# A small first transfer ahead of the large loads, with its results stored in mid-run

## The chip, the cores and the metric

The kernel runs on one core of a Trainium2 chip. The metric is the device time of one execution in microseconds (us). Each kernel was run several times, always beside runs of the kernel before on the same chip. A difference in time under 2% is called a difference only where its 95% interval leaves out 1. The span of a profile is shorter than the device time of the same run (before: 161.4 and 162.92 us).

## The reference

```python
# x: (32, 512, 1024) float32, 67.1 MB
def reference(x):
    relu_x = np.maximum(x, 0)
    return np.sum(relu_x, axis=-1).astype(np.float32)    # (32, 512)
```

There are 16384 rows of 4 KB. Each gives one output number, 4 bytes. Almost all the work is reading 67.1 MB.

## The kernel before

Partition `p` owns 128 consecutive rows, `128 p` to `128 p + 127`. They are loaded in seven large transfers of 16 rows a partition (8 MB each) into three buffers, then a tail of 8, 4, 2 and 1 rows and two half rows. All transfers are issued from one sequencer (SP) and so stand in one queue, served by 16 DMA engines.

```python
xv = x.rearrange("b s d -> (b s) d").rearrange("(p j) d -> p j d", p=P)     # P = 128
ov = out.rearrange("b s -> (b s)").rearrange("(p j) -> p j", p=P)
...                                                                         # cut: buffers, semaphores
for c in range(NBIG + 1):                    # NBIG = 7 large loads, NB = 3 buffers
    if c >= NB:
        sp.wait_ge(s_dve, 3 * (c - NB + 1))  # the buffer's last use is over
    if c < NBIG:
        sp.dma_start(out=buf[:, c % NB, :, :],
                     in_=xv[:, c * BIG : (c + 1) * BIG, :]).then_inc(s_in[c], 16)
...                                          # cut: tail loads of 8, 4, 2, 1 rows and two half rows
                                             # cut: ScalarE does relu, VectorE sums; late rows are
                                             #      done whole on one engine or the other
sp.wait_ge(s_tdve, 1)
sp.dma_start(out=ov[:, :], in_=res[:, :]).then_inc(s_out, 16)   # 128 pieces of 512 bytes
sp.wait_ge(s_out, 16)
```

Of the kernel before, what the change touches and what calls it, by code (L numbers as in the profile page):

```python
# [2 lines left out]

P = 128
D = 1024
BIG = 16
NBIG = 7
NTWO = 6
NB = 3
STEPS = [4, 5, 7]  # L10
MIXED = [3, 4, 5]
TAIL = [8, 4, 2, 1]
LAST = [512, 512]


def bass_relu_sum_kernel(
    nc: bass.Bass,
    x: bass.AP,
    out: bass.AP,
):  # L20





    fp32 = mybir.dt.float32
    ALU = mybir.AluOpType
    AF = mybir.ActivationFunctionType
    X = mybir.AxisListType.X

    B, S, _ = x.shape
    J = B * S // P
    assert BIG * NBIG + sum(TAIL) + 1 == J and sum(LAST) == D

    xv = x.rearrange("b s d -> (b s) d").rearrange("(p j) d -> p j d", p=P)
    ov = out.rearrange("b s -> (b s)").rearrange("(p j) -> p j", p=P)

    buf = nc.alloc_sbuf_tensor("buf", [P, NB, BIG, D], fp32)
    last = nc.alloc_sbuf_tensor("last", [P, LAST[1] + 1], fp32)
    res = nc.alloc_sbuf_tensor("res", [P, J], fp32)  # L40

    n_in = NBIG + len(TAIL) + 2
    s_in = [nc.alloc_semaphore(f"s_in{i}") for i in range(n_in)]
    s_act = nc.alloc_semaphore("s_act")
    s_dve = nc.alloc_semaphore("s_dve")
    s_tact = nc.alloc_semaphore("s_tact")
    s_tdve = nc.alloc_semaphore("s_tdve")
    s_out = nc.alloc_semaphore("s_out")

    sp, act, dve = nc.sync, nc.scalar, nc.vector  # L50


    tb = NBIG % NB
    for c in range(NBIG + 1):
        if c >= NB:
            sp.wait_ge(s_dve, 3 * (c - NB + 1))
        if c < NBIG:
            sp.dma_start(  # L58
                out=buf[:, c % NB, :, :], in_=xv[:, c * BIG : (c + 1) * BIG, :]
            ).then_inc(s_in[c], 16)  # L60
    r = 0
    tail = []
    for i, n in enumerate(TAIL):
        sp.dma_start(  # L64
            out=buf[:, tb, r : r + n, :],
            in_=xv[:, NBIG * BIG + r : NBIG * BIG + r + n, :],
        ).then_inc(s_in[NBIG + i], 16)
        tail.append((r, n, s_in[NBIG + i]))
        r += n
    sp.dma_start(  # L70
        out=buf[:, tb, r, 0 : LAST[0]], in_=xv[:, J - 1, 0 : LAST[0]]
    ).then_inc(s_in[-2], 16)
    sp.dma_start(out=last[:, 0 : LAST[1]], in_=xv[:, J - 1, LAST[0] : D]).then_inc(
        s_in[-1], 16
    )


    def on_act(t, acc):
        return act.activation(t, t, AF.Relu, accum_out=acc)  # L79

    def on_dve(t, acc):
        return dve.tensor_scalar(  # L82
            out=t, in0=t, scalar1=0.0, scalar2=None, op0=ALU.max, op1=ALU.add, accum_out=acc
        )

    def row(c, i):
        return buf[:, c % NB, i, :], res[:, c * BIG + i : c * BIG + i + 1]

    for c in range(NTWO):
        b, steps = c % NB, STEPS if c < NTWO - 1 else MIXED  # L90
        act.wait_ge(s_in[c], 16)
        if steps is MIXED:
            dve.wait_ge(s_in[c], 16)
            for i in (BIG - 4, BIG - 3):
                on_dve(*row(c, i))
        r = 0
        for i, n in enumerate(steps):
            t = buf[:, b, r : r + n, :]
            act.activation(t, t, AF.Relu).then_inc(s_act, 1)  # L99
            dve.wait_ge(s_act, 3 * c + i + 1)  # L100
            dve.tensor_reduce(  # L101
                out=res[:, c * BIG + r : c * BIG + r + n], in_=t, axis=X, op=ALU.add
            ).then_inc(s_dve, 1)
            r += n
        if steps is MIXED:
            for i in (BIG - 2, BIG - 1):
                on_act(*row(c, i))


    j0 = NBIG * BIG  # L110
    for c in range(NTWO, NBIG):
        act.wait_ge(s_in[c], 16)
        dve.wait_ge(s_in[c], 16)
        for i in range(BIG):
            (on_act if i % 2 else on_dve)(*row(c, i))
    for r, n, s in tail:
        if n > 1:
            act.wait_ge(s, 16)
        dve.wait_ge(s, 16)
        for i in range(r, r + n):  # L120
            f = on_act if (i - r) % 2 else on_dve
            f(buf[:, tb, i, :], res[:, j0 + i : j0 + i + 1])

    act.wait_ge(s_in[-2], 16)
    on_act(buf[:, tb, BIG - 1, 0 : LAST[0]], last[:, LAST[1] : LAST[1] + 1]).then_inc(s_tact, 1)
    dve.wait_ge(s_tact, 1)
    dve.wait_ge(s_in[-1], 16)
    on_dve(last[:, :], res[:, J - 1 : J]).then_inc(s_tdve, 1)


    sp.wait_ge(s_tdve, 1)
    sp.dma_start(out=ov[:, :], in_=res[:, :]).then_inc(s_out, 16)
    sp.wait_ge(s_out, 16)


# [1 line left out]
_INS = ['x']  # L137
_OUTS = [((32, 512), 'float32')]


# [21 lines left out]
```

## Time and profile before

| | before |
|---|---|
| time, median of 6 runs beside the changed kernel's | 162.87 us (162.65 to 163.22) |
| span of the profile | 161.4 us |
| share of the 16 DMA engines' time that is busy | 97.0% |
| VectorE, ScalarE busy | 76%, 63% |
| one 64 KB packet on one DMA engine, usual | 2.418 us |
| the 16 engines' first packets start | 1.73 to 2.97 us |
| last load lands (its 16 engines, first to last) | 158.05 to 158.92 us |
| last store, from issue to landing | 1.54 us |

These numbers come from the results, from the page, and from two kinds of records in the trace: packets (a packet is one piece that one DMA engine moves) and semaphore steps. A transfer's landing is 16 semaphore steps, one an engine, and it counts only when the last has come. Landings here and below are read from those steps; of a store they are called its confirmations. No view of the profile prints single packets and steps; a packet record doesn't name its engine, and an engine's first packets are told by which packet follows on which.

From the page of the kernel before: busy time of the compute engines, the DMA row (busy share in 40 equal slices, in tenths), what the DMA engines moved in each slice, and the queue with its packets, MB and share of 16 engines' time.

```profile
DVE 122.0 (76%) x56; ACT 101.0 (63%) x55; POOL 0.2 (0%) x4
...
DMA  7969979979979979979979979979979979899992
GB/s 260 504 292 504 471 341 487 487 325 487 487 325 487 471 309 520 471 309 520 487 309 504 487 325 487 487 325 487 487 325 487 487 325 487 374 422 414 406 406 74
...
q1 hardware_dynamic: 2016, 67.18, 97.0%
```

The DMA engines hardly pause from the first slice to the last. The GB/s row jumps up and down because a packet is counted in the slice in which it starts; three slices (12.1 us) together are steady. In the middle the kernel moves 16 x 65536 bytes / 2.418 us = 434 GB/s. The Trainium skill ("DMA: Bandwidth & Descriptors", Specifications) gives 435 GB/s as the ceiling of the fabric on the side of SBUF (the on-chip memory that the loads go to); the trace agrees.

From the chain of waits of the kernel before in order of time (start, duration, what):

```profile
1.16 41.26 DMA buf<-in_x_dram
...
64.16 36.40 DMA buf<-in_x_dram
...
124.16 34.13 DMA buf<-in_x_dram
158.29 0.02 issue
158.31 0.73 ACT buf L79 x2
159.04 0.02 issue
159.07 0.69 DVE last L82 x2
```

A DMA step in this chain runs from a transfer's issue to its landing and so contains the time in which it waited in the queue. The piece of 36.40 us is the fifth large load, which lands at 100.56 us.

From the DMA issues of the same kernel (KB, then us from issue to landing; for the seven large loads the median, which holds their wait in the queue too):

```profile
buf<-in_x_dram SPq DMA_DIRECT2D x7, 36.4
out_dram<-res SPq DMA_DIRECT2D x1, 64.0 KB, 1.5
```

### The profile page before, as it was taken

The numbers are of one execution on the slowest core, as the hardware profiler recorded it, in microseconds if no ns is written. First come the engines' busy times: TensorE is split into PE (matmuls) and PEld (weight loads), VectorE is DVE, ScalarE is ACT, GpSimd is POOL, SyncE is SP. The second block draws the span as 40 slices with busy tenths as digits, with TensorE's granted clock in tenths as the row PEclk, the third lists the DMA queues.
The fourth block names the chain that finished last, engine by engine and source line by source line (L and its number), as shares of the span: only waits on it lengthen the run. The fifth ranks groups of instructions, "written<-read, shape, count | busy, mean of one in ns | idle before, by whom it ended". The sixth has DMA issues, their size and how long they took to land.

```text
span 161.4 us, 143 instructions
## 1 busy us (share of the span) xinstructions
DVE 122.0 (76%) x56; ACT 101.0 (63%) x55; POOL 0.2 (0%) x4
## 2 busy tenths in 40 slices
DVE  0000003998969898798979989699899999598995
ACT  3000029992499906998089960999429980496972
POOL 0000000000000000000000000000000000000000
DMA  7969979979979979979979979979979979899992
GB/s 260 504 292 504 471 341 487 487 325 487 487 325 487 471 309 520 471 309 520 487 309 504 487 325 487 487 325 487 487 325 487 487 325 487 374 422 414 406 406 74
DMA packets 2016, 67.18 MB, mean 416 GB/s; under 512 B 224, under 2 KB 352, under 8 KB 736
## 3 DMA queue, kind: packets, MB, share of 16 engines
q1 hardware_dynamic: 2016, 67.18, 97.0%
HBM read 67.11 MB, written 0.07 MB: 416 GB/s over the span
## 4 chain that ended last, share of the span: by engine, by line
DMA 69%; ACT 18%; DVE 10%; SPq 1%; issue 0%
DMA buf<-in_x_dram 69%; ACT buf L99 17%; DVE res L101 9%; SPq L64 1%; ACT buf L79 0%; DVE last L82 0%; SPq L58 0%
## 5 line engine op out<-in xcount | busy, mean ns | idle before, releaser
L101 DVE TENSOR_REDUCE res<-buf 128x4 f32<-128x4096 f32 (+3 forms) x18 | 100.4, 5603 | 34.9 <-ACT buf L99 34.9
L99 ACT ACTIVATE buf<-buf 128x4096 f32<-128x4096 f32 (+3 forms) x18 | 80.8, 4553 | 47.7 <-DMA buf<-in_x_dram 47.7
L79 ACT ACTIVATE buf<-buf 128x1024 f32<-128x1024 f32 (+1 forms) x18 | 18.4, 1021 | 9.7 <-DMA buf<-in_x_dram 9.7
L82 DVE TENSOR_SCALAR_CACHE_REDUCE buf<-buf 128x1024 f32<-128x1024 f32 x18 | 21.0, 1217 | 2.7 <-DMA buf<-in_x_dram 2.5
L79 ACT ACTIVATION_READ_ACCUMULATOR buf<-buf 128x1 f32 x18 | 3.4, 187 | 0.0
L99 ACT ACT_TABLE_LOAD x1 | 1.3, 1283 | 0.7 <-PEq L147 0.7
L82 DVE DVE_READ_ACCUMULATOR buf<-buf 128x1 f32 x18 | 1.5, 84 | 0.0
L82 DVE TENSOR_SCALAR_CACHE_REDUCE last<-last 128x513 f32<-128x513 f32 x1 | 0.7, 690 | 0.2 <-ACT buf L79 0.2
L147 POOL MEMSET const-bfloat16-1.0<- 128x1 bf16 x1 | 0.1, 102 | 0.0
L147 POOL MEMSET const-uint8-127<- 128x1 uint8 x1 | 0.1, 101 | 0.0
L147 POOL MEMSET const-float32-0.0<- 128x1 f32 x1 | 0.1, 99 | 0.2 <-issue 0.2
L147 POOL MEMSET const-float32-1.0<- 128x1 f32 x1 | 0.1, 98 | 0.0
L82 DVE DVE_READ_ACCUMULATOR last<-last 128x1 f32 x1 | 0.1, 83 | 0.0
## 6 DMA issues: line engine op xcount, KB each, us to landing
buf<-in_x_dram SPq DMA_DIRECT2D x1, 4096.0 KB, 26.7
buf<-in_x_dram SPq DMA_DIRECT2D x1, 2048.0 KB, 31.2
buf<-in_x_dram SPq DMA_DIRECT2D x1, 1024.0 KB, 33.2
buf<-in_x_dram SPq DMA_DIRECT2D x1, 512.0 KB, 34.0
buf<-in_x_dram SPq DMA_DIRECT2D x1, 256.0 KB, 34.1
last<-in_x_dram SPq DMA_DIRECT2D x1, 256.0 KB, 34.3
buf<-in_x_dram SPq DMA_DIRECT2D x7, 36.4
out_dram<-res SPq DMA_DIRECT2D x1, 64.0 KB, 1.5
```

Of the source, the lines that this page charges most:

```text
L64: sp.dma_start(out=buf[:, tb, r : r + n, :], in_=xv[:, NBIG * BIG + r : NBIG * BIG + r + n, :],).then_inc(s_in[NBIG + i], 16)
L79: return act.activation(t, t, AF.Relu, accum_out=acc)
L82: return dve.tensor_scalar(out=t, in0=t, scalar1=0.0, scalar2=None, op0=ALU.max, op1=ALU.add, accum_out=acc)
L99: act.activation(t, t, AF.Relu).then_inc(s_act, 1)
L101: dve.tensor_reduce(out=res[:, c * BIG + r : c * BIG + r + n], in_=t, axis=X, op=ALU.add).then_inc(s_dve, 1)
L147: nc = _bacc.Bacc("TRN2", target_bir_lowering=False, num_devices=1)
```

## The change

The plan was made for the two ends of the run, since the DMA engines are busy in between: the engines start over 1.2 us, not together. The intent is to begin with a small transfer (64 pieces of 8 KB, two rows each, four pieces to an engine), so that the engines start sooner and closer together while the large transfer's pieces are prepared behind it. To make room for it, every partition now owns 127 rows, and the last 128 rows of `x` are the lead: two to each of the partitions 32 to 95. Their 128 results are contiguous in the output and are stored in mid-run, ahead of the fourth large load, so that the end of the run has nothing to do with them.

```diff
-TAIL = [8, 4, 2, 1]
+TAIL = [8, 4, 1, 1]
+LEAD = 64
...
-    J = B * S // P
+    J = B * S // P - 1
...
+    xv = xr[0 : P * J, :].rearrange("(p j) d -> p j d", p=P)
+    ov = of[0 : P * J].rearrange("(p j) -> p j", p=P)
+    xl = xr[P * J :, :].rearrange("(p j) d -> p j d", p=LEAD)
+    ol = of[P * J :].rearrange("(p j) -> p j", p=LEAD)
...
+    sp.dma_start(out=lead[32:96, :, :], in_=xl[:, :, :]).then_inc(s_lead, 16)
     for c in range(NBIG + 1):
         if c >= NB:
             sp.wait_ge(s_dve, 3 * (c - NB + 1))
+        if c == NB:
+            sp.wait_ge(s_ld, 2)
+            sp.dma_start(out=ol[:, :], in_=lres[32:96, :]).then_inc(s_lout, 16)
...
+    act.wait_ge(s_lead, 16)
+    dve.wait_ge(s_lead, 16)
+    for h in (32, 64):
+        for i, f in enumerate((on_act, on_dve)):
+            ins = f(lead[h : h + 32, i, :], lres[h : h + 32, i : i + 1])
+            if h == 64:
+                ins.then_inc(s_ld, 1)
...                                  # the one-row tail loads: the first goes to ScalarE alone
     sp.wait_ge(s_tdve, 1)
     sp.dma_start(out=ov[:, :], in_=res[:, :]).then_inc(s_out, 16)    # now 127 columns
+    sp.wait_ge(s_lout, 16)
     sp.wait_ge(s_out, 16)
```

The store in mid-run is 64 pieces of 8 bytes, one from each partition.

## The prediction

> **What bounds the kernel.** The DMA engines. The page's queue table gives its one queue 97.0% of 16 engines' time; VectorE is busy 76%, ScalarE 63%. The chain of waits is 69% DMA; where it passes through ScalarE and VectorE (buffers coming free at 44.8 to 122.3 us) a transfer still lies queued behind the running one. The packet records say the same: a 64 KB packet takes 2.418 us on its engine almost every time, 27.1 GB/s an engine, 434 GB/s in all. The Trainium skill ("DMA: Bandwidth & Descriptors", Specifications) states a ceiling of 435 GB/s; the trace agrees, so the middle of the run has nothing to give.
>
> **What is left is the ends.** One engine's share, 64 such packets, is 154.8 us; the span is 161.4.
> - Start: the first issue begins at 0.73 us. The engines start their first packets between 1.73 and 2.97 us, and these take up to 3.27 us, not 2.42. Their ends less 2.42 give effective starts of 2.2 to 3.3 us. The spread lives on: the last load's 16 landings run from 158.05 to 158.92.
> - End: last landing 158.92, ScalarE's half row until 159.04, VectorE's 0.69 us, store issued 159.79, landed 161.3.
>
> With every engine effectively started at 1.8 us, the last landing would come about 1.4 us earlier (estimate from these numbers): under 1%.
>
> **What the change does.** Bytes read are the same.
> 1. The first transfer has 64 descriptors of 8 KB, four an engine (0.309 us each in the tail's records), not 128 of 64 KB. If the stagger comes from making descriptors[...], this starts the engines closer together, and the large transfer's descriptors are made behind it. Estimate: last landing 0.3 to 0.7 us earlier, central 0.5. If the stagger is the first reads' latency, nothing.
> 2. The row pitch falls from 512 to 508 KiB. The skill (same page, Latency and other measured facts) reports copies slowed at pitches of large powers of two; the constant 2.418 us shows no such loss in the steady state, so only the start can gain.
> 3. Lead rows: two passes of about 1.2 us on each engine near 4 to 7 us, when both idle until 23 us: free.
> 4. The store in mid-run: four 8-byte packets per engine, under 0.1 us of queue time (512 B take 27 ns), and one issue of 0.33 us on a sequencer 16 us ahead of need.
> 5. The tail 8,4,1,1 leaves the last landings' order as it was. No change.
> 6. The last store has 508-byte rows. The skill (Specifications) states read-modify-write under 512 B; the 512-byte packets took 27 ns, landing 1.5 us after issue. Estimate: +0.1 to +0.2 us.
>
> Sum: -0.5 + 0.05 + 0.15 = -0.3 us.
>
> **Predicted: 162.55 us** (162.87 before), 161.9 to 163.15. Faster by over 2%: 0.01; within 2%: 0.98; slower: 0.01.
>
> **What would show it.** First packets starting within a narrower stretch than 1.24 us, and the last load landing near 158.4 us. 64 KB packets still at 2.418 us. Lead groups done by about 8 us, with no wait on them later. First large transfer landing about 1.2 us later than 23.1, less the gain. The last store's time to landing above 1.5 us.
>
> **What would make it wrong.** The stagger being latency that the lead inherits (unchanged or +0.2). Large packets opening slowly behind the lead as well. A last store costing over 0.5 us more. Or the 508 KiB pitch disturbing the steady 2.418 us: 1% there is 1.5 us.

## More of the kernel before

From its timeline, the three first issues and the start of ScalarE's work on the fourth large load:

```profile
0.73 1.33 SPq L58 DMA_DIRECT2D buf<-in_x_dram  x3
...
81.25 7.98 ACT L99 ACTIVATE buf<-buf 128x4096 f32<-128x4096 f32 x2 [5.33 <-DMA buf<-in_x_dram]
```

ScalarE begins the fourth load at 81.25 us, 0.03 us after it has landed.

The windows view of 60 to 70 us gives what the DMA engines did there:

```profile
core 0: us, DVE busy (x) ACT busy (x) POOL busy (x), PEclk, DMA share, GB/s
60.00:70.00 10.00, 8.60 (x3) 8.12 (x3) 0.00 (x0) 1.00 0.97 419
```

## The result, and the profile after

The changed kernel takes 164.97 us (median of 6 runs, 164.63 to 165.37), against 162.87 before. Its ratio is 1.0129, with a 95% interval from 1.0111 to 1.0147: 1.3% slower, outside the predicted range. Here and below a ratio is the mean time of one kernel's runs over the mean of the other's of the same rounds, so it is not quite the ratio of the medians.

From the page of the changed kernel, the same lines:

```profile
DVE 123.2 (75%) x58; ACT 103.1 (63%) x59; POOL 0.2 (0%) x4
...
DMA  9699599599799889859989998997997998999991
GB/s 385 256 513 513 256 513 513 256 513 513 305 465 513 385 385 449 321 256 513 513 353 417 513 401 369 513 465 305 513 513 305 465 513 353 409 393 421 437 378 67
...
q1 hardware_dynamic: 2176, 67.18, 96.9%
q14 instruction: 2, 0.02, 0.0%
```

The DMA engines' busy share is the same, 96.9%, and they moved the same bytes, in a longer span. So they were not idle: their packets took longer. Look at the 16th to 18th slices, about 61 to 74 us (449, 321, 256): their mean is 342, where three slices in a row give about 427 for most of the run. A second queue has appeared too, which fetches instructions (two packets of 8 KB); it returns below.

The windows view of 60 to 70 us in the changed kernel:

```profile
60.00:70.00 10.00, 8.67 (x2) 7.31 (x2) 0.00 (x0) 1.00 0.95 315
```

315 GB/s, where it was 419, at a share of 0.95: this is the hole. 104 GB/s over 10 us is 1.04 MB, one round of 16 packets of 64 KB, which at 434 GB/s is 2.4 us. As a packet is counted where it starts, this view shows hardly less than a whole round; the size of the loss is read from landings below.

From the chain of waits of the changed kernel, in order of time:

```profile
2.01 41.28 DMA buf<-in_x_dram
...
65.04 38.69 DMA buf<-in_x_dram
...
125.84 31.20 DMA buf<-in_x_dram
157.04 0.02 issue
157.07 3.96 ACT buf L94 x8
161.03 0.02 issue
161.05 0.69 DVE last L97 x2
```

The first DMA piece is as long as before (41.28, was 41.26); the second is 2.3 us longer (38.69, was 36.40). It lands at 103.73 us in place of 100.56. At the end the chain goes through ScalarE's row work rather than the last load, but that adds nothing: from the last load's landing to the last store's issue is 0.885 us (161.772 - 160.887), and before it was 0.869.

From the DMA issues of the changed kernel:

```profile
lead<-in_x_dram SPq DMA_DIRECT2D x1, 512.0 KB, 3.6
...
buf<-in_x_dram SPq DMA_DIRECT2D x7, 38.7
out_dram<-res SPq DMA_DIRECT2D x1, 63.5 KB, 1.7
out_dram<-lres SPq DMA_DIRECT2D x1, 0.5 KB, 19.2
```

From its timeline, the first issues and ScalarE's start on the fourth large load:

```profile
0.73 0.62 SPq L65 DMA_DIRECT2D lead<-in_x_dram  x1
1.41 1.51 SPq L73 DMA_DIRECT2D buf<-in_x_dram  x3
...
84.40 3.62 ACT L121 ACTIVATE buf<-buf 128x4096 f32<-128x4096 f32 x1 [7.66 <-DMA buf<-in_x_dram]
```

Now the 2.2 us of the span can be laid out, by the times at which transfers land:

| transfer that has landed | before, us | changed, us | difference | what this step added |
|---|---|---|---|---|
| first large load | 23.11 | 23.94 | +0.83 | the lead's bytes came first (32 KB an engine, 1.21 us in a 32 KB packet of the tail): +1.21; so the start gained about 0.38 |
| third large load | 61.85 | 62.67 | +0.82 | nothing |
| fourth large load, behind the store | 81.22 | 84.38 | +3.15 | **+2.33** |
| seventh large load | 139.25 | 142.43 | +3.18 | nothing |
| last load | 158.92 | 160.89 | +1.96 | the tail is shorter by the lead's bytes: -1.21 |
| last store | 161.34 | 163.52 | +2.18 | +0.02 before its issue, +0.20 in the store |

So the lead works as intended, and the store in mid-run loses six times what it gains. In the packet records, the store's 64 packets are processed between 61.85 and 62.32 us and take 9 ns each. But their writes are confirmed only from 62.37 to 64.84 us, and the 64 KB packets behind them are slow: the 16 that start from 64.29 to 66.06 us take 3.25 to 4.70 us in place of 2.42. The last of these end near 69.4 us.

### The profile page after: what moved, and what is told of

The parts are those of the page before. It is cut to its first block, busy times and chain, and to the rows that moved or that the text cites. A ratio compares the mean times of both kernels' runs of the same rounds, so it can differ in the third digit from the quotient of the medians.

```text
span 163.6 us, 152 instructions
## 1 busy us (share of the span) xinstructions
DVE 123.2 (75%) x58; ACT 103.1 (63%) x59; POOL 0.2 (0%) x4
## 3 DMA queue, kind: packets, MB, share of 16 engines
q1 hardware_dynamic: 2176, 67.18, 96.9%
## 4 chain that ended last, share of the span: by engine, by line
DMA 68%; ACT 20%; DVE 10%; SPq 1%; issue 0%
DMA buf<-in_x_dram 68%; ACT buf L121 17%; DVE res L123 9%; ACT buf L94 2%; DVE last L97 0%; SPq L65 0%; SPq L73 0%; SPq L79 0%
## 5 line engine op out<-in xcount | busy, mean ns | idle before, releaser
L97 DVE TENSOR_SCALAR_CACHE_REDUCE buf<-buf 128x1024 f32<-128x1024 f32 x17 | 19.8, 1215 | 2.7 <-DMA buf<-in_x_dram 2.7
L97 DVE TENSOR_SCALAR_CACHE_REDUCE lead<-lead 32x1024 f32<-32x1024 f32 x2 | 2.4, 1210 | 4.4 <-DMA lead<-in_x_dram 4.4
L94 ACT ACTIVATE lead<-lead 32x1024 f32<-32x1024 f32 x2 | 2.1, 1054 | 2.4 <-DMA lead<-in_x_dram 2.4
```

The lines of the kernel that those rows point to most:

```text
L94: return act.activation(t, t, AF.Relu, accum_out=acc)
L97: return dve.tensor_scalar(out=t, in0=t, scalar1=0.0, scalar2=None, op0=ALU.max, op1=ALU.add, accum_out=acc)
```

## The experiments

Theory A: the 64 small pieces stall the loads behind them. Theory B: the loss comes with the layout (127 rows a partition, a pitch of 508 KiB), and the store only stands beside it. If A holds, what about the store is it: small pieces in either direction, any write among reads, or small writes that are crowded together? All runs gave correct results except those that were made wrong on purpose (e7, e11, e14, e15, e16), as said there.

| run | fourth large load lands, us | last load lands, us | last store, issue to landing, us | time, us (median) | ratio to before |
|---|---|---|---|---|---|
| before | 81.22 | 158.92 | 1.54 | 162.87 | 1 |
| after | 84.38 | 160.89 | 1.74 | 164.97 | 1.0129 |
| e1_store_last | 82.00 | 158.54 | 2.90 | 164.29 | 1.0074 |
| e2_before_store | 84.20 | 161.89 | 1.54 | 165.70 | 1.0161 |
| e3_tiny_load | 82.90 | 159.42 | 2.74 | 164.46 | 1.0086 |
| e4_wide_store | 82.19 | 158.78 | 3.77 | 164.44 | 1.0088 |
| e7_no_lead_store | 82.01 | 158.64 | 1.85 | 162.42 | 0.9968 |
| e5_spread | 81.16 | 158.86 | 1.55 | 162.99 | 1.0003 |
| e8_16rows | 82.37 | 160.10 | 1.54 | 163.96 | 1.0060 |
| e6_lead128 | 82.10 | 158.61 | 1.55 | 162.74 | 0.9982 |
| e9_spread64 | 81.14 | 158.86 | 1.54 | 163.07 | 0.9996 |
| e10_whole_lines | 82.10 | 159.63 | 1.90 | 163.27 | 1.0013 |
| e11_store508 | 81.31 | 158.99 | 1.55 | 163.03 | 0.9992 |
| e12_lead128_again | 82.27 | 158.79 | 1.55 | 162.87 | 0.9983 |
| e14_after_spread | 81.98 | 158.52 | 2.29 | 163.23 | 1.0024 |
| e13_waits12 | 81.35 | 159.02 | 1.55 | 162.91 | 0.9995 |
| e15_packed508 | 81.26 | 158.95 | 1.59 | 162.99 | 0.9998 |
| e16_apart508 | 82.01 | 158.85 | 1.58 | 162.67 | 0.9978 |

The landings are those of one profiled execution, the times are of all. In e1 the profiled execution was the fastest of its kernel (163.71 us), in e2, e4, e7, e8 and e10 the slowest (165.94, 164.80, 162.76, 164.19 and 163.84 us), so landings and times need not add up.

In kernels with a lead the fourth large load would land at 82.0 us without a stall, in those without one at 81.2, since the lead's bytes come first.

### e1_store_last: the store behind the last load

```diff
-        if c == NB:
-            sp.wait_ge(s_ld, 2)
-            sp.dma_start(out=ol[:, :], in_=lres[32:96, :]).then_inc(s_lout, 16)
...   # after the last load's issue:
+    sp.wait_ge(s_ld, 2)
+    sp.dma_start(out=ol[:, :], in_=lres[32:96, :]).then_inc(s_lout, 16)
```

> The changed kernel with its one edit: the store of the lead rows' results is issued behind the last load, not ahead of the fourth large load. Theory A (the store's own packets stall the loads behind them, 2.3 us): the landing of the fourth large load comes back to about 82.0 us from 84.4, the last load lands near 158.5, the last store still lands 1.7 us after its issue; time 162.5 to 162.8. Theory B (the loss comes from the 508 KiB row pitch or from the rest of the layout, and the store only happens to lie beside it): the stretch near 62 to 68 us stays slow and the time stays at 164.5 or more.

The hole in mid-run is gone. The windows view of 60 to 70 us in this kernel:

```profile
60.00:70.00 10.00, 8.70 (x2) 7.33 (x2) 0.00 (x0) 1.00 0.97 419
```

The fourth load landed at 82.00 us and the last at 158.54, 0.38 us ahead of the kernel before. Theory B falls. But the time was 164.29 us (ratio 1.0074), not 162.5 to 162.8, so the expectation failed at the end of the run. From the SP queue's own waits, the wait for the last store in the kernel before, then in this one:

```profile
SPq L133 <- DMA out_dram<-res: 1.2, 1, 1.2
```

```profile
SPq L157 <- DMA out_dram<-res: 2.6, 1, 2.6
```

The store costs at the end of the run too: without it (e7, below) the last store took 1.85 us, not 2.90, and the ratio was 0.9968. The small writes were confirmed as late as 159.78 us, and an 8 KB instruction fetch that started just then took 1.76 us; in the profiles with no small store near them such fetches take 0.31 to 0.51 us. Of the last store's 128 packets, 120 had begun by 160.58 us; the other 8, one engine's share, came from 161.53 us, when that fetch ended.

### e2_before_store: the kernel before with such a store

```diff
+        if c == NB:
+            dst = out.rearrange("b s -> (b s)")[P * J - 128 :].rearrange("(p j) -> p j", p=64)
+            sp.dma_start(out=dst, in_=res[32:96, 0:2]).then_inc(s_mid, 16)
```

> The kernel before, with one store of 64 rows of 8 bytes added ahead of its fourth large load (the last store overwrites what it wrote, so the result is right). Theory A: about +2.3 us, time near 165.1, with the slow 64 KB packets just behind the store. Theory B (508 KiB pitch needed): under +0.3 us, near 163.

The ratio is 1.0161 (165.70 us, more than the expected 165.1). From its timeline and its window of 60 to 70 us:

```profile
84.22 3.62 ACT L103 ACTIVATE buf<-buf 128x4096 f32<-128x4096 f32 x1 [8.14 <-DMA buf<-in_x_dram]
```

```profile
60.00:70.00 10.00, 8.46 (x2) 7.96 (x3) 0.00 (x0) 1.00 1.01 315
```

The fourth load lands 2.98 us late (84.20 - 81.22) with nothing of the lead and with the old pitch. The store alone does it. The profile is of the slowest run; by the ratio over all runs the store costs 2.6 us (0.0161 x 163).

### e3_tiny_load: a load of 64 small pieces in its place

```diff
 # e1, and in mid-run:
+            src = xr[0, 0:128].rearrange("(p j) -> p j", p=LEAD)
+            sp.dma_start(out=spare[32:96, :], in_=src).then_inc(s_mid, 16)
```

> As e1, with a LOAD of 64 rows of 8 bytes in the place in mid-run where the store was. If what hurts is a transfer of 64 tiny descriptors in the queue, whatever its direction: the same +2 us over e1, about 164.7. If what hurts is writing to HBM: within 0.2 us of e1.

By the time alone the second line of the expectation would hold: 164.46 us is 0.17 above e1's 164.29, and the intervals overlap. But both kernels carry a disturbed last store, and the landings say more: the fourth load lands at 82.90 us and the last at 159.42, both 0.9 us later than in e1. From its timeline:

```profile
82.93 3.62 ACT L125 ACTIVATE buf<-buf 128x4096 f32<-128x4096 f32 x1 [6.25 <-DMA buf<-in_x_dram]
```

Small crowded reads cost something in this trace, but less than half of what the small crowded writes cost. Whether they would be free 64 bytes apart was not tried.

### e4_wide_store: a store of 64 whole rows of 512 bytes

```diff
 # e1, and in mid-run:
+            dst = of[0 : LEAD * 128].rearrange("(p j) -> p j", p=LEAD)
+            sp.dma_start(out=dst, in_=lead[32:96, 0, 0:128]).then_inc(s_mid, 16)
```

> As e1, with a store of 64 rows of 512 bytes (whole, aligned, 32 KB in all; overwritten by the last store) in mid-run. If any write among the reads stalls the engines (turning round from reading to writing): +2 us over e1, about 164.7. If it is that the writes are pieces of 8 bytes, eight to each 64 bytes: under +0.4 us over e1.

64 times the bytes, the same number of pieces, the same direction: the fourth load lands 0.19 us later than in e1 (82.19, was 82.00), and 0.16 of that was there already in the third load, ahead of the store (62.80, was 62.65). From its timeline:

```profile
82.22 7.97 ACT L125 ACTIVATE buf<-buf 128x4096 f32<-128x4096 f32 x2 [5.35 <-DMA buf<-in_x_dram]
```

The time, 164.44 us, is again e1's, with its disturbed end. So it is not the turn from reading to writing. These 64 pieces adjoin too: whole pieces of 512 bytes may.

### e7_no_lead_store: the lead without its store

```diff
 # e1, without the store of lres and the wait for it (the last 128 outputs are not written)
```

> The changed kernel without any store of the lead rows' results: 128 of the outputs are wrong on purpose. It prices the lead and the 508-byte last store alone. In e1 the last load landed at 158.54 us (before: 158.92), but the last store took 2.9 us to land, while the 64 small writes had landed as late as 159.78 and an 8 KB instruction fetch on one DMA engine had taken 1.76 us. If the small writes had clogged what came after: the last store lands 1.6 to 1.8 us after its issue, and the time is 162.5 to 162.9. If it is the instruction fetch alone: it stays near 2.9 us and the time near 164.

162.42 us, ratio 0.9968 (0.9954 to 0.9982). The lead by itself makes the kernel 0.3% faster, about 0.5 us: what the prediction gave to the lead. The time is just under the expected 162.5 to 162.9. In the profile, of the slowest run, the last store still took 1.85 us (expected 1.6 to 1.8); see the last four runs.

### e5_spread: the pieces 1024 bytes apart

```diff
 # e2 with
-            dst = out.rearrange("b s -> (b s)")[P * J - 128 :].rearrange("(p j) -> p j", p=64)
+            dst = of.rearrange("(p j) -> p j", p=64)[:, 0:2]
```

> The kernel before with a mid-run store of 64 rows of 8 bytes as in e2, but each row 1024 bytes from the next, not all in 512 bytes. If the stall in e2 (fourth large load landing at 84.2 us, before: 81.2) comes from many pieces written to the same few 64-byte lines: it shrinks to under 1 us, time under 163.8. If each piece of under 512 bytes costs by itself wherever it goes: again near +3 us on that landing, time near 165.7.

From its timeline:

```profile
81.18 7.97 ACT L104 ACTIVATE buf<-buf 128x4096 f32<-128x4096 f32 x2 [5.45 <-DMA buf<-in_x_dram]
```

The stall is gone altogether: 81.16 us for the fourth load, ratio 1.0003 (0.9987 to 1.0018). 64 pieces of 8 bytes are free here when they lie apart.

### e8_16rows: 16 pieces

```diff
 # e2 with
+            dst = of[P * J - 32 :].rearrange("(p j) -> p j", p=16)
+            sp.dma_start(out=dst, in_=res[32:48, 0:2]).then_inc(s_mid, 16)
```

> The kernel before with a mid-run store of 16 rows of 8 bytes (one for each DMA engine, contiguous) in the place of e2's 64. If the pieces are served one after the other, the cost goes with their number: about a quarter of e2's 3 us on the fourth large load's landing, time near 163.6. If one write behind the reads stalls each engine once, whatever the number: near 3 us again.

From its timeline and its window of 60 to 70 us:

```profile
82.40 7.98 ACT L104 ACTIVATE buf<-buf 128x4096 f32<-128x4096 f32 x2 [6.67 <-DMA buf<-in_x_dram]
```

```profile
60.00:70.00 10.00, 8.68 (x3) 8.31 (x3) 0.00 (x0) 1.00 1.10 419
```

The fourth load lands at 82.37 us, 1.15 late, and the time is 163.96 us (ratio 1.0060; expected near 163.6). A quarter of the pieces costs 1.15 / 2.98 = 39% of the stall. The cost grows with the number of pieces, but it is not proportional to it. The window shows 419 GB/s, as without a stall: a loss of less than one round of packets doesn't show there.

### e9_spread64: the pieces 64 bytes apart

```diff
 # e2 with
+            dst = of[0:1024].rearrange("(p j) -> p j", p=64)[:, 0:2]
```

> The kernel before with the mid-run store of 64 rows of 8 bytes, now 64 bytes from one row to the next (4 KB in all), between e2 (8 bytes apart: +3 us) and e5 (1024 bytes apart: nothing). Theory A2 (the stall comes from several pieces in one 64-byte line): as e5, the fourth large load lands within 0.3 us of 81.2, time 162.8 to 163.2. Rival (it comes from all pieces lying close together, in one small stretch of memory): over +1 us on that landing, time 164 or more.

From its timeline and its window of 60 to 70 us:

```profile
81.16 7.97 ACT L104 ACTIVATE buf<-buf 128x4096 f32<-128x4096 f32 x2 [5.29 <-DMA buf<-in_x_dram]
```

```profile
60.00:70.00 10.00, 8.66 (x3) 8.17 (x3) 0.00 (x0) 1.00 0.98 419
```

At 64 bytes apart, within 4 KB, there is no stall (ratio 0.9996). So closeness in a few KB is not enough to stall; the pieces must be closer than 64 bytes. Only distances of 8, 64 and 1024 bytes were tried. Where between 8 and 64 bytes it begins is open. Here and in e5 the pieces also go to another place in the output than in e2; e10 keeps the place.

### e10_whole_lines: the same 512 bytes in two pieces

```diff
+    for h in (32, 64):                       # VectorE turns the results into rows of one partition
+        for i in (0, 1):
+            dve.transpose(tr[h : h + 32, i, :], lr[h : h + 32, i, :]).then_inc(s_tr, 1)
+    dve.wait_ge(s_tr, 4)
+    for h in (32, 64):
+        dve.tensor_copy(rows[h : h + 1, :].rearrange("o (j i) -> o i j", i=2),
+                        tr[h : h + 1, :, :]).then_inc(s_ld, 1)
...
+            for g, h in enumerate((32, 64)):     # in mid-run: two pieces of 256 bytes
+                sp.dma_start(out=of[P * J + 64 * g : P * J + 64 * (g + 1)]
+                             .rearrange("(o j) -> o j", o=1),
+                             in_=rows[h : h + 1, :]).then_inc(s_lout, 16)
```

> The changed kernel, lead unchanged, but VectorE first turns the lead's 128 results into two rows of 64 in one partition each, so that the mid-run store is two pieces of 256 whole bytes to the same 512 bytes, in the same place in the queue. If the pieces were the fault and not the place or the bytes: the fourth large load lands at 82.0 us as in e1, not 84.4, and the time is 162.3 to 162.8. If any early write to that place costs: 164 or more.

From its timeline:

```profile
82.12 7.98 ACT L141 ACTIVATE buf<-buf 128x4096 f32<-128x4096 f32 x2 [5.35 <-DMA buf<-in_x_dram]
```

The same bytes to the same place at the same time, in two pieces: the fourth load lands at 82.10 us, so the stall is gone, and the result is correct. The time, 163.27 us, missed its 162.3 to 162.8. The profile is of the slowest run, 0.57 us over that median. In it the last load landed at 159.63 us, 1.09 later than in e1. From about 76 to 128 us some packets in every 4 us took 2.45 to 2.68 us. An instruction fetch ran at 145.9 us, and after it the last of the 16 engines landed 0.47 us behind the one before it, where it had been 0.02 to 0.12 behind. The fetch coincides with that and was not tested; the slow packets have no explanation.

### e6_lead128 and e12_lead128_again: a lead that needs no second store

```diff
 # the kernel before, with a lead of one row for each of the 128 partitions
+    sp.dma_start(out=lead[:, :], in_=xv[:, 0, :]).then_inc(s_lead, 16)
...  # its result is column 0 of res and leaves with the last store; the rest is shifted by one row
+    dve.wait_ge(s_lead, 16)
+    on_dve(lead[:, :], res[:, 0:1])
```

> The kernel before with a lead of one row for each of the 128 partitions (128 descriptors of 4 KB, pitch 512 KiB), whose results leave with the last store in rows of 512 bytes: no second store. If a short first transfer is what narrows the start: the last load lands about 0.4 us sooner than 158.92, the last store lands 1.5 us after issue, time near 162.4. If the gain needs the dense 64-descriptor lead or the other pitch: the first packets start over more than 1 us as before, and the time is 162.8 to 163.2.

> e6 once more, on the same chip as e10, to set the two versions without the small pieces side by side. Its last load landed at 158.61 us and its last store took 1.5 us, so 162.4 to 162.8; e10 should be 0 to 0.3 us slower, for its 508-byte store and longer program.

The first packets start between 1.74 and about 2.2 us (e6), the last load lands at 158.61 and 158.79 us, and the last store takes 1.55 us in both. The ratios are 0.9982 (0.9969 to 0.9995) and 0.9983 (0.9968 to 0.9998). This correct version beats both kernels, by 0.2% against the kernel before; both intervals leave out 1. It keeps the pitch of 512 KiB and starts at the same addresses as the kernel before, so the gain at the start does not need the other pitch, other addresses or the 64 pieces. The expectations missed in part: the times are over 162.4 (e6) and just over 162.8 (e12), and e10 was 0.4 us slower than e12, not 0 to 0.3. In e12 the medians (162.87, and 163.10 for the runs of the kernel before beside it) show why small differences are read only within the same rounds.

### e14_after_spread: the changed kernel with its store's pieces apart

```diff
-            sp.dma_start(out=ol[:, :], in_=lres[32:96, :]).then_inc(s_lout, 16)
+            dst = of[0:1024].rearrange("(p j) -> p j", p=LEAD)[:, 0:2]
+            sp.dma_start(out=dst, in_=lres[32:96, :]).then_inc(s_lout, 16)
```

> The changed kernel with only the addresses of its mid-run store changed: the 64 pieces of 8 bytes go 64 bytes apart, into a stretch that the last store overwrites (so the last 128 outputs are left unwritten on purpose and the result is wrong); same number of pieces, same place in the queue, same program length but for the order of two waits. If the crowding of the pieces is the whole of the loss: the fourth large load lands at 82.0 us, not 84.4, and the time is 162.3 to 162.8, as in e7. If something else in the mid-run store costs (pieces, issue, write among reads): above 163.3.

From its timeline:

```profile
82.01 7.97 ACT L122 ACTIVATE buf<-buf 128x4096 f32<-128x4096 f32 x2 [5.31 <-DMA buf<-in_x_dram]
```

From its DMA issues (in the changed kernel this store took 19.2 us from issue to landing):

```profile
out_dram<-lres SPq DMA_DIRECT2D x1, 0.5 KB, 17.1
```

With the pieces set apart (and so in another place, which e10 shows not to be what counts), the fourth load is back at 81.98 us and the last load at 158.52. The 16 confirmations of the small store now all come within 0.52 us of its last packet (62.815 - 62.291); crowded, it was 2.52 us (64.84 - 62.32). That settles the loss in mid-run in the changed kernel itself. The time is 163.23 us (ratio 1.0024), not 162.3 to 162.8, with runs from 162.67 to 164.09: here the last store took 2.29 us. So part of the expectation missed, at the other end of the run.

### e11, e13, e15, e16: the last store

```diff
 # e11: the kernel before; rows of 508 bytes, 512 apart (last column not written)
+    sp.dma_start(out=ov[:, 0 : J - 1], in_=res[:, 0 : J - 1]).then_inc(s_out, 16)
 # e13: the kernel before, twelve met waits more on the sequencer that issues
+            for _ in range(12):
+                sp.wait_ge(s_in[0], 16)
 # e15: the kernel before; rows of 508 bytes one directly after the other (wrong on purpose)
+    dst = out.rearrange("b s -> (b s)")[0 : P * (J - 1)].rearrange("(p j) -> p j", p=P)
 # e16: e7; rows of 508 bytes, 512 apart (wrong on purpose)
+    dst = of.rearrange("(p j) -> p j", p=P)[:, 0:J]
```

> The kernel before, its last store cut to 127 columns (508-byte pieces, 512 apart; the last column of the output is left unwritten on purpose, so the result is wrong). It prices the shorter rows of the last store without the longer program. If rows of 508 bytes are what made the changed kernel's last store land 1.74 us after issue and not 1.54: again 1.7 us. If it was the instruction fetch that ran beside that store on one DMA engine: 1.5 to 1.6 us, time within 0.1 us of before.

> The kernel before with twelve already met waits added to the issuing sequencer's program, ahead of its fourth large load, and nothing else. In the changed kernel the last store landed 1.74 us after its issue (before: 1.54) while an 8 KB instruction fetch ran on the DMA engines just behind that issue; e11 showed that the 508-byte rows are not the cause. If the longer program brings that fetch under the last store and the fetch delays it: landing 1.7 to 1.9 us after issue and time 0.1 to 0.3 us over before. If not: 1.54 us and the same time.

> The kernel before, its last store as 128 rows of 508 bytes laid one directly after the other, as in the changed kernel (in e11 they stood 512 apart and cost nothing); the result is wrong on purpose. Program length as before, no instruction fetch near the end. If rows that share a 64-byte line with their neighbour are what slows the last store: landing 1.7 us or more after issue, varying, time +0.2 us or more. If it is the fetch: 1.54 us and the time of before.

> e7 (the changed kernel without the lead's store) with its last store's rows of 508 bytes set 512 apart, so that no two share a line; wrong on purpose. The program's length and its late instruction fetches stay. If shared lines slowed e7's last store (1.85 us after issue): 1.5 to 1.6 us here and time 162.2 to 162.4. If the fetches did: 1.7 us or more, time as e7.

Shorter rows cost nothing (e11: 1.55 us from issue to landing). Packed rows without a late instruction fetch cost next to nothing (e15: 1.59 us, ratio 0.9998). A late fetch beside rows that stand apart costs next to nothing either (e16: 1.58 us, with a fetch at 160.1 us). (The times of e16 missed their 162.2 to 162.4.) e13 decided nothing: the longer program of that sequencer brought no fetch under the last store. Either twelve waits are too few or the fetch belongs to another engine's program; no run shows which. All four profiled kernels with a slow last store and no small store near it (the changed kernel 1.74, e7 1.85, e10 1.90, e14 2.29) had packed rows and a late fetch together. Whether the two act together or the last store of these kernels merely scatters is open. The times don't decide it: e16 was at 0.9978, no better than e7 at 0.9968.

## Why the prediction was wrong

**The bound (right).** The DMA engines bound both kernels, usual 64 KB packets stayed at 2.418 to 2.420 us, and only disturbed ones took longer.

**Step 1, the lead (right, at the low end of its size).** The engines' first packets now start between 2.13 and 2.46 us, over 0.33 us where it was 1.23. In e1, e7 and e14 the last load landed 0.28 to 0.40 us earlier than before; the prediction said 0.3 to 0.7, central 0.5. In e16, with the same lead, it was 0.08: there 0.42 was still gained at the fourth load, and slow packets lost it by the seventh. The prediction had missed one thing: the lead's issue takes 0.62 us where the first issue before took 0.38, and its first packet starts 0.4 us later than before (2.13, was 1.73), which eats part of the gain. The large packets behind the lead also opened slowly (2.48 to 3.10 us), as the prediction had warned. That a short first transfer narrows the start is shown (e6 too); why it does, whether by its descriptors or otherwise, no run separates.

**Step 2, the pitch (right as far as seen).** The steady packets show no difference at 508 KiB, and e6 has the gain at 512 KiB. The skill's remark on pitches of large powers of two ("DMA: Bandwidth & Descriptors", Latency and other measured facts) tells of copies with pitches of 512 KiB and more; no run here shows such a loss.

**Step 3, the lead's compute (right).** Both engines had finished with it before 7 us and next worked at 23.96 us or later.

**Step 4, the store in mid-run (the step that failed).** The prediction called it "under 0.1 us of queue time", reasoning from the packets' time. The packets did take 9 ns each. But the loads behind them were held for 2.33 us (changed kernel) and 2.98 us (e2). None of the things that the prediction listed as what could make it wrong was this store. What was priced was how long a DMA engine handles a small piece. The loss went instead with the time from the store's last packet to its last confirmation: 0.43 to 0.87 us where the fourth load was not held (e4, e5, e9, e14), 1.15 in e8, 2.52 in the changed kernel and 3.07 in e2, where it was held for 1.15, 2.33 and 2.98. Which of the two brings the other about is not shown. e14 and e9 show that for pieces of 8 bytes adjoining is the condition: 64 bytes apart, the same pieces are free. e10 shows it from the other side: the same 512 bytes in two pieces are free. Not tried: pieces between 8 and 256 bytes that adjoin, adjoining pieces all written by one DMA engine, and the same store from another queue.

The skill (same page, Specifications) states that for a transfer under 512 bytes the DMA engine does a read-modify-write (the old bytes are read, changed and written back). The prediction used this for the last store, where short rows cost nothing (e11), and did not use it for the store of 8-byte pieces. As a rule on size alone it would not have helped: e5 and e9 write pieces of 8 bytes without loss. That several pieces have to update the same unit of memory, one after the other, would fit the runs with stores (e3's reads, which update nothing, lost 0.9 us all the same), but no run shows what the memory does, and this is argued only.

**Step 5, the tail (right).** 0.885 us from the last landing to the last store's issue, against 0.869.

**Step 6, the last store (size right by luck, reason wrong).** Predicted +0.1 to +0.2 us for rows of 508 bytes; measured +0.20. But e11 shows that rows of 508 bytes cost nothing by themselves. The cause of the +0.20 is open.

The sum of the prediction was -0.5 + 0.05 + 0.15. Read from the landings and stores, it was -0.38 + 2.33 + 0.02 + 0.20 = +2.17 us, within 0.01 of the measured +2.18 at the last store.

## What to carry to other kernels

Price a small store by the time until its writes are confirmed, not by the time its packets take, and look at where its pieces go: results of a few bytes that sit in many partitions but adjoin in memory were the bad case in this stream of loads. Gather them into one partition (e10: no stall, but no gain in time either), let them leave with a store of long rows (e6, the only version that was both correct and faster), or choose the rows so that the pieces lie apart. In the profile such a stall does not show as idle DMA time: the busy share stays near full while GB/s falls, so compare GB/s over equal windows, and for a loss of less than one round of packets (e8) compare when the loads land.

## What the Trainium skill lacked or had wrong

- "DMA: Bandwidth & Descriptors" (Specifications; Why small descriptors are slow) speaks of the size of a piece. It lacks the distance between pieces: 64 writes of 8 bytes held the loads behind them for 2.33 to 2.98 us when they adjoined, and for nothing at 64 or 1024 bytes apart (fourth load at 81.14 and 81.16 us, before 81.22). Rows of 508 bytes, under the stated 512, landed in 1.55 us as against 1.54.
- The same page (Anatomy of one DMA) describes another way of issuing than this kernel's and puts most of a transfer's fixed cost down to confirming the write. It lacks the split for this way. Of the last store's 1.54 us (before), 0.84 passed before its first packet and 0.35 between its last packet and its last confirmation, so here the confirmation was not most of it. It also lacks that this part can grow while loads behind are slow: 0.52 to 0.87 us from the last packet to the last confirmation with pieces of 8 bytes apart (e14, e9, e5), 2.52 and 3.07 us with 64 adjoining ones (changed kernel, e2).
- No page that was read here gives the issue time of a transfer by its shape on this chip: 0.62 us for the lead's 64 rows as first transfer and 0.56 for the large one behind it, against 0.37 and 0.42 with 128 rows (e6); a store of 16 rows took 0.36 (e8), of 64 rows 0.59 (e2); a later large load took 0.33.
- "Runtime: NRT & Kernel Launch" (Instruction fetch mechanics) tells that a sequencer fetches its instructions through its own DMA queue, in blocks of 16 KiB. It lacks what a fetch costs beside data: here it shows as packets of 8 KB, which took 0.31 to 0.51 us in most runs and, the first of them, 1.67 to 2.71 us just behind adjoining small writes (e1, e3, e4), where one engine's share of the last store came only as the fetch ended.
